# A decoder trunk's attention passes: both groups of scores at the head of a pass, in banks exchanged with the transposes

## The chip, the cores and the metric

One NeuronCore of a Trainium2 chip runs the whole kernel in one launch. Its engines are called here as in the profile: PE (TensorE; its weight loads are PEld), DVE (VectorE), ACT (ScalarE), POOL (GpSimd) and SP (SyncE, which issues loads). The metric is the device time of one execution in microseconds (us), as the median of several. Each engine works through its own queue in order, and an instruction waits at the head of its queue until its semaphores have come.

## What is computed

Two decoder layers on 512 tokens of width 1024 in float32. The first has a gated short convolution, the second sliding-window attention with sinks; each is followed by a SwiGLU block. The change concerns the attention alone: 16 heads of 64, four key heads, and each block of 128 queries sees its own block of keys and the one before.

```python
q = (rmsnorm(h, b_pre_norm[j]) @ b_w_q[j]).reshape(bsz, s, N_HEADS, HEAD_DIM)
q = partial_rotary(q, cos, sin)
attn = sliding_window_sink_attention(q, k_sh, v_sh, b_sinks[j]) @ b_w_o[j]
...
scores = jnp.einsum('bnqhgd,bnkhd->bnhgqk', qb, kk).astype(jnp.float32) * scale
scores = jnp.where(valid[None, :, None, None], scores, NEG)
probs = jax.nn.softmax(jnp.concatenate([scores, sink], axis=-1), axis=-1)[..., :-1]
out = jnp.einsum('bnhgqk,bnkhd->bnqhgd', probs.astype(v.dtype), vv)
```

## The kernel before

Every float32 product is made of three matmuls: each operand is split into a high part (ACT copies it to a shorter float) and a low part (DVE subtracts the high part from the original), and high by low, high by high and low by high are summed in PSUM.

Attention runs over eight head pairs, software-pipelined. The loop at line 1447 makes passes i = 0 to 9, and in each it walks through one string, `ORDER` (line 47). Within the loop the order on PE, DVE, ACT and POOL is the order of the program; a step issues instructions on several engines, and each lands at the end of that engine's queue. A letter is a step, the digit behind it a part of it, and "-" means that it belongs to the pass before. The steps, with pair t = i unless said otherwise:

- R- and H- (pair i + 1): rotate the queries. R: DVE shuffles (`sh`) and multiplies (`ra`), POOL multiplies and adds (lines 1211 to 1215). H: ACT makes the high part `rhi`, POOL the low part `rlo` (lines 1220, 1221). Behind both, POOL issues DMAs that add weight blocks in memory for the next layer (line 535).
- Q0 to Q3 (pair i + 2): project the queries, 6 matmuls of 512 columns each, into one PSUM bank `pq`.
- S0, S1: the scores of two groups of two query blocks each, 12 matmuls with 64-row operands, into two banks `psc` per group (line 1273).
- M0, M1: DVE adds the mask and takes the row maxima, four operations a group (line 1285). The banks of the group are free when these have read them.
- E00, E01, E10, E11: ACT's exponents with row sums (line 1301), and the sink's (line 1308).
- N0, N1: DVE adds sums and sink, takes the reciprocal and scales four pieces (lines 1313 to 1318). The first two pieces of group 0 are 128 wide, the others 256.
- T0 to T3 (pair i - 1): PE transposes the scaled rows into a bank `pt` (line 1330). T0 reads group 0, T1 both groups, T2 and T3 group 1.
- P and L (pair i - 1): ACT's high part `phi` and DVE's low part `plo` of a `pt` bank (lines 1343, 1347).
- W0 to W3 (pair i - 1): weigh the values, 6 matmuls each, into one bank `po`. W of j needs P and L of j.
- O- (pair i - 2): ACT and DVE split the weighed values (`ohi`, `olo`).
- G (pair i + 3): load and split the query weights of a later pair, or, from pass 5 on, of the output projection: ACT makes `whi`, DVE `wlo`, in one step (lines 173 to 188). g0 and g1 do the same for more weights of the output projection, in passes 4 and 6.
- Z and z: from pass 5 on, PE makes two units of the output projection per pass from pairs that are done, and ACT takes their banks.
- K: in pass 2 only, the rotation of the second half of the keys (DVE, POOL, ACT, POOL as for the queries).
- A: in pass 8 only, weights of the next block.

So pass 0 has no T, P, L, W; passes 1 to 5 project queries; passes 6 and 7 don't, but have Z; pass 8 has no scores.

PSUM has eight banks in three pools: four for products (`ps_mm`, with `pq`, `po` and Z), two for the scores (`ps_sc`) and two for the transposes (`ps_pt`). Before the change S0 and S1 both take the two banks of `ps_sc`, so that S1 waits until M0 has read them, and the four transposes take the two banks of `ps_pt` by turns.

Of the kernel before, what the change touches and what calls it, by code (L numbers as in the profile page):

```python
# [10 lines left out]
F32 = mybir.dt.float32  # L11
F32R = mybir.dt.float32r
AF = mybir.ActivationFunctionType
ALU = mybir.AluOpType
PSUM = bass.MemoryType.PSUM

P = 128
D = 1024
S = 512
KT = D // P  # L20
F = 2816
# [23 lines left out]

EARLY_IN, REST_IN = 2, 0
ORDER = (
    "R- T0 g0 S0 O- T1 Q0 M0 Q1 Z0 P0 P1 S1 T2 L0 Q2 L1 G M1 E00 E01 T3 H- Q3 P2 P3 E10 E11 Z1 z0 K W0 L2 L3 A A A N0 W1 W2 N1 W3 g1 z1"
)
STEP = {  # L50
    "S": "scores", "M": "maxima", "E": "exponents", "N": "normalise", "T": "turn", "P": "high",
    "L": "low", "W": "weigh", "O": "out", "Q": "project", "R": "rotate", "H": "split",
    "G": "weights", "Z": "project", "z": "out",
}
N_SLOT, N_WIDE, N_RAW, N_W = 43, 14, 7, 4
EARLY = 4
# [16 lines left out]
def yoco_kernel(  # L73
# [22 lines left out]
    nc = tc.nc  # L96
# [6 lines left out]
    wsp = ctx.enter_context(tc.tile_pool(name="wsp", bufs=N_W))  # L103
# [3 lines left out]
    ps_sc = ctx.enter_context(tc.tile_pool(name="ps_sc", bufs=2, space=PSUM))  # L107
    ps_pt = ctx.enter_context(tc.tile_pool(name="ps_pt", bufs=2, space=PSUM))
# [3 lines left out]
    def name(s):  # L112
        uid[0] += 1
        return f"{s}_{uid[0]}"
# [13 lines left out]
    def bank(s, pool=None):  # L128

        if pool is None:  # L130
            pool = (ps_mm, ps_sc, ps_mm, ps_pt)[turn[0] % 4]
            turn[0] += 1
        return pool.tile([P, S], F32, tag="bank", name=name(s))
# [21 lines left out]
    def fetch(src, n=D):  # L155
        raw = wraw.tile([P, D], F32, tag="raw", name=name("raw"))
        dst = raw[:, :n]
        if len(src.shape) == 3:
            src, dst = src.rearrange("k p c -> p k c"), dst.rearrange("p (k c) -> p k c", c=S)
        nc.sync.dma_start(dst, src)  # L160
        return raw

    class Two:
# [5 lines left out]
        def __getitem__(self, at):  # L169
            h = at[1].start // S  # L170
            return self.of[h][:, at[1].start - h * S : at[1].stop - h * S]

    def split_weights(src, raw=None, slots=False):
        if raw is None:
            raw = fetch(src)
        if slots:
            hi, lo = Two("whi", F32R), Two("wlo", F32R)
            for h in range(2):
                c = slice(h * S, (h + 1) * S)
                nc.scalar.activation(hi[:, c], raw[:, c], AF.Copy)  # L180
                nc.vector.tensor_tensor(out=lo[:, c], in0=raw[:, c], in1=hi[:, c].bitcast(F32),
                                        op=ALU.subtract)
            return hi, lo
        hi = wsp.tile([P, D], F32R, tag="whi", name=name("whi"))
        lo = wsp.tile([P, D], F32R, tag="wlo", name=name("wlo"))
        nc.scalar.activation(hi, raw, AF.Copy)
        nc.vector.tensor_tensor(out=lo, in0=raw, in1=hi.bitcast(F32), op=ALU.subtract)
        return hi, lo
# [468 lines left out]
    with tc.manual_schedule(engines=ALL):  # L657
# [25 lines left out]
        for k in range(KT):  # L683
            pieces = FIRST.get(k, [])
# [6 lines left out]
            for i in range(3):  # L691
                for t in range(3):
                    n = 3 * k + t
                    whi, wlo = (w[:, n % KT * P : (n % KT + 1) * P] for w in ws[n // KT])
# [21 lines left out]
        for b in range(NB):  # L716
            nc.vector.tensor_scalar(out=dg[:, b * P : (b + 1) * P], in0=ident,
                                    scalar1=cols[:, b : b + 1], scalar2=None, op0=ALU.mult)
# [506 lines left out]
    class Queries:  # L1225
# [2 lines left out]
            self.ps = None  # L1228

        def weights(self):  # L1230
            self.w = split_weights(w_q[self.t])

        def project(self, part):
            if part == 0:
# [12 lines left out]
    class Heads:  # L1247
# [11 lines left out]
        def scores(self, half):  # L1259
            khi, klo = ks[self.t // 4]  # L1260
            qhi, qlo = qs[self.t].hi, qs[self.t].lo
            self.pss[half] = pss = [bank("psc", ps_sc) for _ in range(2)]
            for i, cc in self.spans(half):
                n = 2 * half + i
                q = slice(n * P, (n + 1) * P)

                kk = slice(max(n - 1, 0) * P, max(n + 1, 2) * P)
                cc = slice(i * 256, (i + 1) * 256)
                rows = [slice(e * HD, (e + 1) * HD) for e in range(2)]

                for i, (x, y) in enumerate(((qhi, klo), (qhi, khi), (qlo, khi))):
                    for e, r in enumerate(rows):
                        nc.tensor.matmul(pss[e][:, cc], x[r, q], y[r, kk], start=i == 0,
                                         stop=i == 2)
# [35 lines left out]
        def normalise(self, half):  # L1310
            se, rs = self.sums[half]
            pe = self.pe[half]
            nc.vector.tensor_tensor(out=se, in0=se, in1=rs, op=ALU.add)
            rd = small.tile([P, 2, 2], F32, tag="rd", name=name("rd"))
            nc.vector.reciprocal(out=rd, in_=se)
            for i, cc in self.spans(half):
                for e in range(2):
                    nc.vector.tensor_scalar(
                        out=pe[e][:, cc], in0=pe[e][:, cc], scalar1=rd[:, e, i : i + 1],
                        scalar2=None, op0=ALU.mult,  # L1320
                    )

        def turn(self, j):
            pt = bank("pt", ps_pt)
            nq = 2 if j < NB - 1 else 1
            for e in range(2):
                for typ in range(nq):
                    n = j + typ
                    c = (n % 2) * 256 + (P if typ == 0 and n > 0 else 0)
                    nc.tensor.transpose(  # L1330
                        pt[:, (e * nq + typ) * P : (e * nq + typ + 1) * P],
                        self.pe[n // 2][e][:, c : c + P], ident,
                    )
            if nq == 2:
                phi, plo = slot("phi", F32R), slot("plo", F32R)
                self.turned[j] = phi, plo, pt, phi, plo
            else:
                view = [p.rearrange("p (e c) -> p e c", e=2)[:, :, P:] for p in last_p]
                self.turned[j] = *last_p, pt[:, :256].rearrange("p (e c) -> p e c", e=2), *view
# [46 lines left out]
    early_w, rest_w = [], []  # L1386
# [5 lines left out]
    with tc.manual_schedule(engines=ALL):  # L1392
        last_tile(res, [[(0, 4)], [(0, 5)], [], [(0, 6), (0, 7), (1, 0), (1, 1)],
                        [(1, f) for f in (4, 5, 2, 3, 6, 7)]])
        for hf in range(2):
            c = slice(hf * 256, (hf + 1) * 256)
# [41 lines left out]
        src = [p.rearrange("p (h d) -> p h d", d=HD) for p in pv]  # L1438
        for j in range(NB):
            nc.scalar.activation(dst[j][0], src[j], AF.Copy)  # L1440
        for j in range(NB):
            nc.vector.tensor_tensor(out=dst[j][1], in0=src[j], in1=dst[j][0].bitcast(F32),
                                    op=ALU.subtract)

    with tc.manual_schedule(engines=ALL):
        sum_on("a0")
        for i in range(KT + 2):
            if i == KT:
                res = Update(mix_o, B_ATT, [G_FPRE[1]])
                res.leaves = True  # L1450
                ahead = Ahead(first_weights(1))
            if i == KT + 1:
                res.load()
            for c in ORDER.split():
                if c == "A":
                    if i == KT:
                        ahead.one()
                    continue
                if c == "K":
                    if i == 2:  # L1460
                        ks.append(rope_split(rope(pk[1], nc.gpsimd), nc.gpsimd))
                    continue
                late = c.endswith("-")
                op, n = c[0], [int(d) for d in c[1:].rstrip("-")]
                t = i - late
                if op == "g":

                    u = 2 * (t - EARLY - 1) + n[0]
                    if u in (-2, -1, 2, 3):
                        j = u + 2 if u < 0 else u  # L1470
                        early_w.append(split_weights(w_o[j // 2, j % 2], slots=j >= EARLY_IN))
                    continue
                if op in "SMENTPLWO":
                    t -= op in "TPLWO"
                    of = hp
                elif op in "QRH":
                    t += LEAD
                    of = qs
                elif op == "G":
                    t += LEAD + 1  # L1480
                    of = qs
                    if KT <= t < KT + 4:
                        j = t - KT
                        rest_w.append(split_weights(w_o[j // 2, 2 + j % 2], slots=j >= REST_IN))
                else:
                    t = 2 * (t - EARLY - 1) + n.pop(0)
                    of = early
                if 0 <= t < len(of) and not (op in "RH" and t < LEAD - 1):
                    getattr(of[t], STEP[op])(*n)
                if op in "RH" and i <= KT:  # L1490
                    issue(len(issues) // 2 if op == "R" else len(issues))
            if i <= KT:
                sum_on(f"a{i + 1}")
        close(rest_w, at, EARLY, res, ahead, lambda: sum_on(f"a{KT + 2}"), 1)
# [96 lines left out]
```

## Time and profile before

| | us |
|---|---|
| median of 3 runs | 1027.31 (1027.06 to 1027.46) |
| the profiled execution | 1027.09 |
| its span in the trace | 1025.3 |
| PE busy / DVE / ACT / POOL | 1016.4 / 823.7 / 577.4 / 195.8 |
| attention passes 0 to 8 in the span | about 550 to 660 |

The span is what the trace covers, from the first instruction to the last; the profiled execution's own time is 1.8 us more. In rows of the trace in order of time, the columns are start (us from the span's start), duration, engine, line, operation, output and inputs by the program's names, their shapes, a count of merged instructions, and in brackets the idle time of the engine before, with what ended it. Neighbouring instructions of an engine overlap, since they are pipelined: the time that one takes of its engine is read from start to start. PE's ends are modelled, so on PE only starts are used. In rows of stretches the columns are the stretch, its length, busy time and count of PE, PEld, DVE, ACT and POOL, the granted clock, the DMA share and GB/s. In rows of waits they are who waited, for what, the total in us, the times and the longest.

### The profile page before, as it was taken

Reading aid. Unit: us, or ns where it says so; the run is one execution under the profiler, and the core shown is the slowest. Engines: PE = TensorE matmul, PEld = TensorE weight load, DVE = VectorE, ACT = ScalarE, POOL = GpSimd, SP = SyncE. Lnnn points to the kernel's source line nnn. Section 1 sums busy time; section 2 is a strip of 40 time slices with the busy share of each in tenths; the row PEclk is TensorE's granted clock in tenths of the full one; section 3 lists DMA queues with packets and bytes.
Section 4 is the critical chain, followed back from the end, with each engine's and each line's share of the span. In section 5 each row is a group of like instructions: output and inputs, shape, how many; then the busy total and the mean of one; then the engine's idle time right before and its main releaser. Section 6 shows DMA issues by size and latency. Waiting matters only on the chain.

```text
span 1025.3 us, 17466 instructions
## 1 busy us (share of the span) xinstructions
PE 1016.4 (99%) x6648; PEld 925.8 (90%) x6648; DVE 823.7 (80%) x1400; ACT 577.4 (56%) x1035; POOL 195.8 (19%) x259
## 2 busy tenths in 40 slices
PE   9999999999999999999999999999999999999997
PEld 8888888999899898998897888889998999989986
DVE  5766767888688879878869998778886788887786
ACT  7323445865655454566476776677665554645642
POOL 0433033111111111000123653231111010110001
PEclk9999999999999999999999999999999999999999
DMA  9897699459978699779404789976889576988732
GB/s 353 293 268 224 181 255 350 135 169 291 338 246 291 200 313 319 254 220 307 164 9 156 186 246 268 233 280 153 275 282 326 167 263 208 311 286 259 243 135 83
DMA packets 66580, 244.59 MB, mean 239 GB/s; under 512 B 7872, under 2 KB 8384, under 8 KB 54720
## 3 DMA queue, kind: packets, MB, share of 16 engines
q1 hardware_dynamic: 51328, 145.98, 39.0%
q0 software_dynamic: 14592, 96.48, 36.7%
q8 instruction: 52, 0.85, 0.3%
q10 hardware_dynamic: 576, 1.02, 0.3%
q14 instruction: 32, 0.26, 0.1%
HBM read 237.15 MB, written 102.76 MB: 332 GB/s over the span
## 4 chain that ended last, share of the span: by engine, by line
PE 94%; DVE 4%; ACT 1%; DMA 1%; issue 0%; DVEq 0%; SPq 0%
PE gx L193 7%; PE gx L192 7%; PE gx L191 7%; PE gz L192 4%; PE gz L193 4%; PE gz L191 4%; PE pcub L191 4%; PE pcub L193 4%; PE pcub L192 4%; PE px L191 4%; PE px L192 4%; PE px L193 4%; PE pmix L193 3%; PE pmix L191 3%; PE pmix L192 3%; PE gy L191 2%
## 5 line engine op out<-in xcount | busy, mean ns | idle before, releaser
L467 DVE TENSOR_TENSOR wlo<-raw,whi 128x1024 fp32r<-128x1024 f32 x225 | 275.3, 1227 | 93.3 <-ACT whi L466 93.1
L466 ACT ACTIVATE whi<-raw 128x1024 fp32r<-128x1024 f32 x225 | 234.2, 1049 | 118.2 <-DVE raw L454 20.4
L192 PE MATMUL gx<-xt,whi 128*128 128x256 f32 x480 | 135.9, 283 | 0.0
L193 PE MATMUL gx<-xt,wlo 128*128 128x256 f32 x480 | 135.9, 283 | 0.0
L191 PE MATMUL gx<-xt,whi 128*128 128x256 f32 x480 | 135.9, 283 | 0.0
L192 PEld LDWEIGHTS gx<-xt,whi 128*128 128x128 f32 x480 | 92.2, 192 | 0.0
L193 PEld LDWEIGHTS gx<-xt,wlo 128*128 128x128 f32 x480 | 92.2, 192 | 0.0
L191 PEld LDWEIGHTS gx<-xt,whi 128*128 128x128 f32 x480 | 92.2, 192 | 0.0
L535 POOL DMA_DIRECT2D hsum<-in_w_gb_dram x96 | 63.5, 741 | 142.0 <-ACT whi L466 82.3
L1001 ACT ACTIVATE st<-gx 128x256 f32<-128x256 f32 x80 | 30.3, 383 | 82.6 <-PE gx L193 82.6
L535 POOL DMA_DIRECT2D hsum<-hsum x32 | 25.2, 789 | 264.3 <-ACT whi L466 209.1
L192 PE MATMUL pcub<-xhi,whi 128*128 128x512 f32 x168 | 65.4, 389 | 0.0
L191 PE MATMUL pcub<-xlo,whi 128*128 128x512 f32 x168 | 65.4, 389 | 0.0
L193 PE MATMUL pcub<-xhi,wlo 128*128 128x512 f32 x168 | 65.4, 389 | 0.0
L191 PE MATMUL px<-wlo,ahi 128*128 128x512 f32 x120 | 46.7, 390 | 0.0
L192 PE MATMUL px<-whi,ahi 128*128 128x512 f32 x120 | 46.7, 389 | 0.0
L193 PE MATMUL px<-whi,alo 128*128 128x512 f32 x120 | 46.7, 389 | 0.0
L192 PE MATMUL gz<-xt,whi 128*128 128x256 f32 x160 | 45.3, 283 | 0.0
L192 PE MATMUL gx<-xhi,whi 128*128 128x256 f32 x160 | 45.3, 283 | 0.0
L191 PE MATMUL gy<-xlo,whi 128*128 128x256 f32 x160 | 45.3, 283 | 0.0
L192 PE MATMUL gy<-xhi,whi 128*128 128x256 f32 x160 | 45.3, 283 | 0.0
L193 PE MATMUL gz<-xt,wlo 128*128 128x256 f32 x160 | 45.3, 283 | 0.0
(268 smaller groups left out, 3119.7 us busy)
## 6 DMA issues: line engine op xcount, KB each, us to landing
hsum<-in_w_gb_dram POOLq DMA_DIRECT2D x96, 512.0 KB, 8.0
raw<-hsum SPq DMA_DIRECT2D x88, 512.0 KB, 7.9
raw<-in_w_gb_dram SPq DMA_DIRECT2D x60, 512.0 KB, 7.5
hsum<-in_w_dn_dram POOLq DMA_DIRECT2D x36, 512.0 KB, 8.7
raw<-in_w_dn_dram SPq DMA_DIRECT2D x32, 512.0 KB, 6.7
hsum<-hsum POOLq DMA_DIRECT2D x28, 512.0 KB, 5.4
raw<-in_w_in_dram SPq DMA_DIRECT2D x21, 512.0 KB, 8.1
hsum<-in_w_dn_dram POOLq DMA_DIRECT2D x12, 768.0 KB, 12.7
```

The source lines that it names most:

```text
L191: nc.tensor.matmul(out, whi, xlo, start=start, stop=False, **kw)
L192: nc.tensor.matmul(out, whi, xhi, start=False, stop=False, **kw)
L193: nc.tensor.matmul(out, wlo, xhi, start=False, stop=stop, **kw)
L466: self.begun = nc.scalar.activation(hi[:, :n], raw, AF.Copy)
L467: nc.vector.tensor_tensor(out=lo[:, :n], in0=raw, in1=hi[:, :n].bitcast(F32), op=ALU.subtract)
L535: nc.gpsimd.dma_start(dst, src, max_dma_last_dim=4 * 4 * S, **kw))
L1001: nc.scalar.activation(s, x, AF.Copy)
```

## The change

In short:

- S0 and S1 stand together at the head of a pass (in pass 0, S1 stays behind Q0 and Q1). S0 takes the banks of `ps_sc` and S1 those of `ps_pt`; T0 and T1 take `ps_sc`, T2 and T3 `ps_pt`.
- Transposes stand in pairs: T0 T1 behind Q0 and Q1, T2 T3 behind Q2.
- G is cut in two: G loads and makes the high part (ACT), now ahead of the exponents; F makes the low part (DVE), now behind L1. M1 stands right behind E01, ahead of g0 and of all L.
- H- moves ahead of the late exponents; L2 and L3 move ahead of K; W1 moves up to W0.
- Of N0, the two 128-wide scalings run on ACT instead of DVE.

No arithmetic is added or left out. The whole diff:

```diff
--- before.py
+++ after.py
@@ -45,12 +45,12 @@
 
 EARLY_IN, REST_IN = 2, 0
 ORDER = (
-    "R- T0 g0 S0 O- T1 Q0 M0 Q1 Z0 P0 P1 S1 T2 L0 Q2 L1 G M1 E00 E01 T3 H- Q3 P2 P3 E10 E11 Z1 z0 K W0 L2 L3 A A A N0 W1 W2 N1 W3 g1 z1"
+    "R- S0 S1 O- G M0 E00 E01 M1 Q0 Q1 g0 T0 T1 P0 P1 L0 L1 F H- Z0 Q2 T2 T3 E10 P2 P3 L2 L3 E11 Q3 Z1 z0 K W0 W1 A A A N0 W2 N1 W3 g1 z1"
 )
 STEP = {
     "S": "scores", "M": "maxima", "E": "exponents", "N": "normalise", "T": "turn", "P": "high",
     "L": "low", "W": "weigh", "O": "out", "Q": "project", "R": "rotate", "H": "split",
-    "G": "weights", "Z": "project", "z": "out",
+    "G": "high_weights", "F": "low_weights", "Z": "project", "z": "out",
 }
 N_SLOT, N_WIDE, N_RAW, N_W = 43, 14, 7, 4
 EARLY = 4
@@ -169,6 +169,23 @@
         def __getitem__(self, at):
             h = at[1].start // S
             return self.of[h][:, at[1].start - h * S : at[1].stop - h * S]
+
+    def split_begun(src, slots):
+        raw = fetch(src)
+        if slots:
+            w = Two("whi", F32R), Two("wlo", F32R)
+            pieces = [slice(h * S, (h + 1) * S) for h in range(2)]
+        else:
+            w = [wsp.tile([P, D], F32R, tag=tag, name=name(tag)) for tag in ("whi", "wlo")]
+            pieces = [slice(0, D)]
+        for c in pieces:
+            nc.scalar.activation(w[0][:, c], raw[:, c], AF.Copy)
+
+        def rest():
+            for c in pieces:
+                nc.vector.tensor_tensor(out=w[1][:, c], in0=raw[:, c],
+                                        in1=w[0][:, c].bitcast(F32), op=ALU.subtract)
+        return w, rest
 
     def split_weights(src, raw=None, slots=False):
         if raw is None:
@@ -1228,7 +1245,14 @@
             self.ps = None
 
         def weights(self):
-            self.w = split_weights(w_q[self.t])
+            self.high_weights()
+            self.low_weights()
+
+        def high_weights(self):
+            self.w, self.rest = split_begun(w_q[self.t], False)
+
+        def low_weights(self):
+            self.rest()
 
         def project(self, part):
             if part == 0:
@@ -1259,7 +1283,7 @@
         def scores(self, half):
             khi, klo = ks[self.t // 4]
             qhi, qlo = qs[self.t].hi, qs[self.t].lo
-            self.pss[half] = pss = [bank("psc", ps_sc) for _ in range(2)]
+            self.pss[half] = pss = [bank("psc", (ps_sc, ps_pt)[half]) for _ in range(2)]
             for i, cc in self.spans(half):
                 n = 2 * half + i
                 q = slice(n * P, (n + 1) * P)
@@ -1315,13 +1339,15 @@
             nc.vector.reciprocal(out=rd, in_=se)
             for i, cc in self.spans(half):
                 for e in range(2):
-                    nc.vector.tensor_scalar(
-                        out=pe[e][:, cc], in0=pe[e][:, cc], scalar1=rd[:, e, i : i + 1],
-                        scalar2=None, op0=ALU.mult,
-                    )
+                    r = rd[:, e, i : i + 1]
+                    if half == i == 0:
+                        nc.scalar.activation(pe[e][:, cc], pe[e][:, cc], AF.Copy, scale=r)
+                    else:
+                        nc.vector.tensor_scalar(out=pe[e][:, cc], in0=pe[e][:, cc], scalar1=r,
+                                                scalar2=None, op0=ALU.mult)
 
         def turn(self, j):
-            pt = bank("pt", ps_pt)
+            pt = bank("pt", (ps_sc, ps_pt)[j // 2])
             nq = 2 if j < NB - 1 else 1
             for e in range(2):
                 for typ in range(nq):
@@ -1451,7 +1477,10 @@
                 ahead = Ahead(first_weights(1))
             if i == KT + 1:
                 res.load()
-            for c in ORDER.split():
+            order = ORDER
+            if i == 0:
+                order = order.replace("S0 S1", "S0").replace("M1 Q0 Q1", "Q0 Q1 S1 M1")
+            for c in order.split():
                 if c == "A":
                     if i == KT:
                         ahead.one()
@@ -1476,12 +1505,16 @@
                 elif op in "QRH":
                     t += LEAD
                     of = qs
-                elif op == "G":
+                elif op in "GF":
                     t += LEAD + 1
                     of = qs
                     if KT <= t < KT + 4:
                         j = t - KT
-                        rest_w.append(split_weights(w_o[j // 2, 2 + j % 2], slots=j >= REST_IN))
+                        if op == "G":
+                            w, rest = split_begun(w_o[j // 2, 2 + j % 2], j >= REST_IN)
+                            rest_w.append(w)
+                        else:
+                            rest()
                 else:
                     t = 2 * (t - EARLY - 1) + n.pop(0)
                     of = early
```

## The prediction

> **What bounds the kernel now.** I read the page first (busy time by engine, the chain that ended last), then the busy time by stretch inside the attention passes, then the waits, then three engines' rows in order of time.
>
> ```profile
> PE 1016.4 (99%) x6648; PEld 925.8 (90%) x6648; DVE 823.7 (80%) x1400; ACT 577.4 (56%) x1035; POOL 195.8 (19%) x259
> PE 94%; DVE 4%; ACT 1%; DMA 1%; issue 0%; DVEq 0%; SPq 0%
> 570.70:582.90 12.20, 12.20 (x89) 10.28 (x87) 12.12 (x35) 8.81 (x28) 8.77 (x8) 1.00 0.90 247
> 570.90:585.55 14.65, 14.58 (x107) 11.98 (x106) 14.50 (x41) 10.34 (x31) 10.06 (x9) 1.00 0.92 241
> 585.55:596.40 10.85, 10.47 (x69) 8.84 (x68) 10.71 (x38) 8.54 (x26) 5.98 (x6) 1.00 0.61 154
> PEld pt L1330 <- DVE s L1318: 1.3, 4, 0.4
> ```
>
> The stretches give length, then busy time of PE, PEld, DVE, ACT, POOL, then the clock. The first is pass 2 as PE lives it (from its first transposes to the next pass's): 12.2 us without a wait at full clock. The next two are passes 2 and 3 as DVE lives them, from one `sh` of the queries to the next: DVE is busy 14.50 of 14.65 us and 10.71 of 10.85. So PE sets the end of the kernel (94% of the chain), but in passes 2 to 4 DVE has nothing to spare. Time that PE saves here reaches the end only if DVE can follow.
>
> PE's time in a pass holds change-overs between the scores (64-row operands), the transposes and the projections. Pass 4, first as it begins, then where a projection meets the scores in pass 0, then two waits:
>
> ```profile
> 596.18 0.60 PE L1330 MATMUL pt<-ident,s 128*128 128x128 f32 x4
> 596.71 0.38 PE L1273 MATMUL psc<-rlo,rhi 64*128 64x256 f32 x2
> 596.93 0.28 PE L1273 MATMUL psc<-rhi,rhi 64*128 64x256 f32 x2
> 597.05 0.28 PE L1273 MATMUL psc<-rhi,rlo 64*128 64x256 f32 x2
> 597.40 0.28 PE L1273 MATMUL psc<-rhi,rlo 64*128 64x256 f32 x2
> 597.61 0.66 PE L1330 MATMUL pt<-ident,s 128*128 128x128 f32 x4
> 598.03 0.48 PE L191 MATMUL pq<-xlo,whi 128*128 128x512 f32 x1
> 598.34 0.40 PE L192 MATMUL pq<-xhi,whi 128*128 128x512 f32 x1
> 598.58 0.40 PE L193 MATMUL pq<-xhi,wlo 128*128 128x512 f32 x1
> ...
> 555.04 0.28 PE L1273 MATMUL psc<-rhi,rlo 64*128 64x256 f32 x2
> 555.24 0.50 PE L191 MATMUL pq<-xlo,whi 128*128 128x512 f32 x1
> 555.58 0.40 PE L192 MATMUL pq<-xhi,whi 128*128 128x512 f32 x1
> ...
> 588.54 0.76 PE L1273 MATMUL psc<-rlo,rhi 64*128 64x256 f32 x2 [0.33 <-DVE nm L1285]
> 601.27 0.76 PE L1273 MATMUL psc<-rlo,rhi 64*128 64x256 f32 x2 [0.22 <-DVE nm L1285]
> ```
>
> From start to start: four transposes take 0.42 us (597.61 to 598.03), but 0.53 ahead of scores (596.18 to 596.71): 0.11. A pair of score matmuls takes 0.12, the first 0.22: 0.10. So scores cost 0.21 going in. Going out, the last pair takes 0.21 ahead of a transpose (0.09), and ahead of a projection 0.20 with the projection's first matmul at 0.34 for 0.24 (0.18 together). The first projection matmul behind transposes takes 0.31 for 0.24 (0.08 with rounding).
>
> [...]
>
> **The change, part by part.** *Change-overs.* Before, a pass of 1 to 5 goes into scores twice and out to transposes twice, and three times from transposes to a projection: 2 x 0.30 + 3 x 0.08 = 0.84. After: in once, out to a projection once, two transposes-to-projection: 0.21 + 0.18 + 0.16 = 0.55. That saves 0.29 in each of five passes. Passes 6 and 7 have no queries to project: 0.76 becomes 0.46, saving 0.30 each. Together 2.0 us. The way from weighing to scores isn't in the trace; between 0 and 0.2 in, I take the same 0.21, as from transposes.
>
> *Waits of PE that go.* Transposes wait for the normalised rows four times, 1.3 us; scores wait for DVE's maxima 0.33 and 0.22, with some 0.3 more each, since their first matmuls run stretched (0.76). About 0.4 in pass 1, 1.0 in pass 3, 0.5 in pass 4, and 0.4 in pass 8, which stays, because pass 8 has no scores or projections to put ahead of T0.
>
> *What is waited for instead.* T0 and T1 now take the banks of S0, free when M0 has read them, 4.55 us after the pass's head (0.21 + 1.40 for 24 score matmuls + 0.18 + 12 x 0.23 for Q0 and Q1); in passes 6 and 7, without Q0 and Q1, 1.7 us after it. T2 and T3 take the banks of S1, freed by M1 well before them. So DVE's place decides. Its pass 3, with ACT's rows that go with it:
>
> ```profile
> 585.55 0.74 DVE L1211 STREAM_SHUFFLE sh<-pq 128x512 f32<-128x512 f32 x1
> 586.18 0.67 DVE L1213 TENSOR_TENSOR ra<-pq,ctab 128x512 f32<-128x512 f32 x1
> 586.78 0.68 DVE L1365 TENSOR_TENSOR olo<-po,ohi 128x512 fp32r<-128x512 f32 x1
> 587.37 0.34 DVE L1285 CUSTOM_DVE_ANT_0 s<-psc,mask,nsnk 128x128 f32<-128x128 f32 x1
> 588.72 1.28 DVE L1347 TENSOR_TENSOR plo<-pt,phi 128x512 fp32r<-128x512 f32 x2
> 589.92 1.22 DVE L187 TENSOR_TENSOR wlo<-raw,whi 128x1024 fp32r<-128x1024 f32 x1
> 591.05 0.48 DVE L1285 CUSTOM_DVE_ANT_0 s<-psc,mask,nsnk 128x256 f32<-128x256 f32 x1
> 592.67 0.68 DVE L1347 TENSOR_TENSOR plo<-pt,phi 128x512 fp32r<-128x512 f32 x1
> 593.61 0.15 DVE L1313 TENSOR_TENSOR se<-se,rs 128x4 f32<-128x4 f32 x1
> 595.34 1.14 DVE L1318 TENSOR_SCALAR s<-s,rd 128x256 f32<-128x256 f32 x4
> ...
> 585.52 0.60 ACT L1343 ACTIVATE phi<-pt 128x512 fp32r<-128x512 f32 x1 [0.98 <-PE pt L1330]
> 586.01 1.05 ACT L186 ACTIVATE whi<-raw 128x1024 fp32r<-128x1024 f32 x1
> 587.76 0.40 ACT L1301 ACTIVATE s<-s,nm 128x128 f32<-128x128 f32 x1 [0.69 <-DVE nm L1285]
> 589.90 0.62 ACT L1220 ACTIVATE rhi<-ra 128x512 fp32r<-128x512 f32 x1
> ```
>
> Start to start: `sh` 0.63, `ra` 0.60, `olo` 0.59, M0 1.35, L 0.60, weights' low part 1.13, M1 1.62, L2 with L3 0.94, N0 with N1 2.79 (to 596.40). The change takes the two 128-wide scalings of N0 off DVE, 0.45, onto ACT, which has room (8.54 busy of 10.85).
>
> *The low part of the weights meets GpSimd.* DVE's operations on two SBUF operands, and its scalings, don't run beside a GpSimd tensor operation:
>
> ```profile
> 597.22 1.27 POOL L1214 TENSOR_TENSOR sh<-sh,stab 128x512 f32<-128x512 f32 x1 [3.93 <-DVE sh L1211]
> 597.62 1.95 DVE L187 TENSOR_TENSOR wlo<-raw,whi 128x1024 fp32r<-128x1024 f32 x1
> 590.60 1.69 POOL L1221 TENSOR_TENSOR rlo<-ra,rhi 128x512 fp32r<-128x512 f32 x1 [0.86 <-ACT rhi L1220]
> 578.12 0.73 DVE L1211 STREAM_SHUFFLE sh<-pk 128x512 f32<-128x512 f32 x1
> 580.26 1.04 DVE L1313 TENSOR_TENSOR se<-se,rs 128x4 f32<-128x4 f32 x1
> 581.56 1.90 DVE L1318 TENSOR_SCALAR s<-s,rd 128x128 f32<-128x128 f32 x4
> ```
>
> `wlo` at 597.62 took 1.95 for 1.22: it began behind `sh` and ran when that had ended. At 590.60 it is the other way round, `rlo` took 1.69 instead of 1.3 behind a `wlo` begun at 589.92. Now count from M0's start: the exponents begin at 0.39 and fill ACT for 2.14 (587.76 to 589.90); P0 ends at 3.13, P1 begins at 3.02 (0.49 apart, 585.52 to 586.01), `rhi` runs from 3.51 to 4.13, `rlo` from 4.20 to 5.50. DVE: M0 and M1 to 2.97, L0 behind P0 from 3.17, L1 from 3.77, the low part F at 4.37, that is 0.17 behind `rlo`. So F is held to 5.50. Bounds: 0 (F first) and 1.3; I take 1.13 in passes 1 to 4. A DVE pass is then 10.85 - 0.45 + 1.13 + 0.2 = 11.7, PE's 11.9.
>
> *K in pass 2.* The keys' rotation (1.22 on DVE, three GpSimd operations of 1.3 with a 0.62 `rhi`) moves behind L2 and L3. Before, it held N0 and N1 up by 0.9 three times (1.04 for 0.15; 1.90 for 1.0; similarly N1), with L2 and L3 as cover. After, DVE comes to pass 2 at 571.8 (570.90 and pass 1's held F, less N0's share); M0 573.6, L1 done 578.0, F 580.2, L3 581.2, K 582.4; GpSimd's three end at 583.3, 584.7 and 586.7, the scalings of N1 at 587.8. Before: 585.55.
>
> *Passes one by one.* Pass 1: -0.3 - 0.4, and W2, which needs L2 behind F, waits 0.6: -0.1. Pass 2: -0.3. Pass 3: T0 is due at 582.4 + 4.55 = 587.0, its bank is free at 587.8 + 1.82 + 1.02 = 590.6: a wait of 3.6, and W2 waits 0.5 for L2; -0.3 - 1.0 + 4.1 = +2.8. Pass 4 (two more weights on DVE): W2 waits 0.8: -0.3 - 0.5 + 0.8 = 0. Pass 5: DVE comes 2.4 behind PE's head, T0 waits 0.6: +0.3. Passes 6 and 7: from the last weighing to the free bank lie `ohi` 0.67, `olo` 0.64 and three reductions 1.02, 2.35 in all; T0 is due at 1.7: +0.65 - 0.3 each, +0.8 with 0.1 for DVE's lag in 7. Pass 8: 0. Sum: -0.1 - 0.3 + 2.8 + 0 + 0.3 + 0.8 = **+3.5 us**. The profiled execution took 1027.09, 0.2 under the median shown, so 1030.6 and for the median **1030.8**. Bounds of pass 3's wait: 0 if DVE arrives as early as PE, 4.5 if POOL's DMA issues (0.5 to 0.8 each) delay K's operations.
>
> **Rivals.** *F wins its race* (0.17 us decides). Then W2's waits go (0.6 + 0.5 + 0.8 = 1.9), DVE leaves pass 2 some 1.9 earlier (0.9 from pass 1, 1.0 from its own F), and pass 5's wait goes (0.6): 4.4 less, 1026.4. For it: the margin is smaller than one reduction. Against: all its terms are steady rows, and the order is the same in each pass. [...]
>
> *DVE follows and the kernel is faster.* M0 and M1 stand ahead of the weights' low part, the transposes' waits are covered and ACT takes 0.45. If T0 never waits, the change-overs (2.0) and the waits (1.9) are gained: 1023.4. It decides where M0's first bank is free within 4.55 us of PE's head in pass 3, and 1.7 in 6 and 7; rows speak against both.
>
> *GpSimd's queue makes the queries late.* `rlo` stands behind DMA issues that wait for sums; S0 now stands at the very head. If one `rlo` comes 2 us late, 1033. Against: `rlo` ends some 4 us before the next head.
>
> **Chances.** Forecast 0.60, F's race 0.24, faster 0.12, GpSimd 0.04. A measurement of this kernel tells about 0.2%, 2.05 us, from no change. Faster 0.12 (the second rival), same 0.24 (the first), slower 0.64. The range runs from 1025.8, which takes in the first rival, to 1032.8; the second and half of the third are left out. The forecast's own range is 1029.0 to 1032.8.
>
> **What would show it.** Change-overs: score groups of 24 without a gap, one 0.34 projection behind them. F: `wlo` of 1.9 to 2.4 us in passes 1 to 4 with `rlo` just ahead. Pass 3: transposes wait over 2 us for maxima. Passes 6 and 7: T0 waits 0.6 or more. Wrong, if `wlo` takes 1.2 and `rlo` waits instead, or if PE goes through pass 3 without a wait over 1 us.

## The result, and the profile after

The changed kernel takes 1031.47 us (median of 5, 1030.9 to 1033.24), the kernel before on the same chip 1027.19 (5 runs, 1027.06 to 1027.46): a ratio of 1.0043, 95% interval 1.0031 to 1.0054. It is 4.3 us slower. The profiled execution took 1030.9, with a span of 1029.1.

The page after: busy time by engine, and the chain that ended last.

```profile
PE 1015.6 (99%) x6648; PEld 928.0 (90%) x6648; DVE 822.4 (80%) x1384; ACT 581.1 (56%) x1051; POOL 193.9 (19%) x259
PE 92%; DVE 6%; ACT 1%; issue 1%; DVEq 0%; ACTq 0%
```

PE is busy for 0.8 us less and still sets the end, but DVE's share of the chain rose from 4% to 6%: PE now waits for DVE somewhere. To find it, cut both executions at the heads of the passes, the first matmul behind the last weighing (T0 before, S0 after). The stretches of passes 2, 3, 4 and 6, before:

```profile
570.72:582.88 12.16, 12.16 (x88) 10.24 (x87) 12.08 (x34) 8.79 (x28) 8.77 (x8) 1.00 0.89 245
582.88:596.18 13.30, 12.85 (x88) 10.55 (x88) 13.09 (x46) 10.09 (x29) 7.27 (x7) 1.00 0.68 159
596.18:608.90 12.72, 12.45 (x88) 10.45 (x87) 12.58 (x40) 9.66 (x28) 8.74 (x9) 1.00 0.75 182
...
626.36:638.34 11.98, 11.98 (x89) 10.30 (x88) 11.84 (x38) 10.51 (x32) 4.44 (x5) 1.00 0.98 232
```

and after:

```profile
571.45:583.20 11.75, 11.75 (x87) 10.37 (x86) 11.67 (x33) 8.36 (x27) 6.81 (x7) 1.00 0.80 216
583.20:599.88 16.68, 13.46 (x89) 11.64 (x88) 16.26 (x47) 10.36 (x32) 8.74 (x9) 0.90 0.66 169
599.88:611.63 11.75, 11.75 (x87) 10.37 (x86) 11.06 (x33) 10.45 (x31) 7.50 (x9) 1.00 0.70 173
...
629.33:641.88 12.55, 11.72 (x87) 10.36 (x87) 11.56 (x36) 12.16 (x36) 4.22 (x6) 1.00 0.87 229
```

Passes 2 and 4 run without a wait, 11.75 us each. Pass 3 takes 3.4 us more than before, and its mean clock is 0.90. All passes, in us, beside the forecast (pass 8 to the next layer's first matmul):

| pass | before | after | difference | forecast |
|---|---|---|---|---|
| 0 and 1 | 20.26 | 20.27 | 0.0 | -0.1 |
| 2 | 12.16 | 11.75 | -0.4 | -0.3 |
| 3 | 13.30 | 16.68 | +3.4 | +2.8 |
| 4 | 12.72 | 11.75 | -1.0 | 0 |
| 5 | 17.46 | 17.70 | +0.2 | +0.3 |
| 6 and 7 | 24.09 | 25.30 | +1.2 | +0.8 |
| 8 | 10.29 | 9.89 | -0.4 | 0 |
| sum | | | +3.1 | +3.5 |

The other 0.7 us of the profiled difference lies ahead of the attention: the first scores of pass 0 start at 550.46 before and at 551.18 after. The last section gives the reason for putting this down to the execution and not to the change.

The 0.0 of passes 0 and 1 hides terms that cancel. In pass 1 the changed kernel's W2 waits 0.28, and T0 waits 0.37 (0.60 from the last projection matmul, which needs 0.23), for which the prediction had no term.

PE in pass 3 after, in order of time, and the clock in three stretches of 4 us:

```profile
587.45 0.39 PE L210 MATMUL pq<-xhi,wlo 128*128 128x512 f32 x1
591.07 1.94 PE L1356 MATMUL pt<-ident,s 128*128 128x128 f32 x8 [3.23 <-DVE nm L1309]
592.66 0.78 PE L208 MATMUL pq<-xlo,whi 128*128 128x512 f32 x1
593.23 0.63 PE L209 MATMUL pq<-xhi,whi 128*128 128x512 f32 x1
593.66 0.63 PE L210 MATMUL pq<-xhi,wlo 128*128 128x512 f32 x1
594.09 0.47 PE L208 MATMUL pq<-xlo,whi 128*128 128x512 f32 x1
```

```profile
587.00:591.00 4.00, 0.84 (x4) 0.38 (x2) 4.00 (x15) 1.53 (x4) 2.26 (x3) 0.98 0.28 78
591.00:595.00 4.00, 3.94 (x16) 3.50 (x17) 3.86 (x13) 4.00 (x15) 1.98 (x3) 0.60 0.60 98
595.00:599.00 4.00, 4.00 (x31) 3.74 (x30) 3.86 (x10) 3.06 (x12) 1.52 (x3) 1.00 0.69 201
```

The transposes T0 and T1 start 3.62 us behind the last projection matmul, which needs 0.23: a wait of 3.39 for the maxima that free the bank. Then the matmuls run at half pace: 1.59 for the eight transposes that take some 0.8 elsewhere, 0.43 for a projection matmul of 0.23. The granted clock, 0.98 ahead, is 0.60 for these 4 us. Pass 3's own sum is 16.68 - 11.75 - 3.39 = 1.54 us for the slow clock.

What DVE did meanwhile, from the weights' low part of pass 2 to pass 3's maxima, and GpSimd beside it:

```profile
578.59 2.21 DVE L186 TENSOR_TENSOR wlo<-raw,whi 128x1024 fp32r<-128x1024 f32 x1
...
581.66 0.73 DVE L1228 STREAM_SHUFFLE sh<-pk 128x512 f32<-128x512 f32 x1
...
582.88 0.96 DVE L1337 TENSOR_TENSOR se<-se,rs 128x4 f32<-128x4 f32 x1
...
584.09 1.51 DVE L1346 TENSOR_SCALAR s<-s,rd 128x256 f32<-128x256 f32 x2
...
585.92 2.25 DVE L1346 TENSOR_SCALAR s<-s,rd 128x256 f32<-128x256 f32 x4
588.09 0.01 DVE L1228 LOAD_MASK_SELECT sh<-pq  x1
...
590.43 0.48 DVE L1309 CUSTOM_DVE_ANT_0 s<-psc,mask,nsnk 128x256 f32<-128x256 f32 x1
```

```profile
578.43 1.28 POOL L1238 TENSOR_TENSOR rlo<-ra,rhi 128x512 fp32r<-128x512 f32 x1 [1.79 <-ACT rhi L1237]
...
582.54 1.29 POOL L1231 TENSOR_TENSOR sh<-sh,stab 128x512 f32<-128x512 f32 x1 [1.27 <-DVE sh L1228]
583.90 1.28 POOL L1232 TENSOR_TENSOR ra<-ra,sh 128x512 f32<-128x512 f32 x1
585.93 1.29 POOL L1238 TENSOR_TENSOR rlo<-ra,rhi 128x512 fp32r<-128x512 f32 x1 [0.74 <-ACT rhi L1237]
```

Read the two side by side. F begins at 578.59, 0.16 behind `rlo`, and takes 2.21 instead of 1.22: it lost its race. K's three GpSimd operations each hold a VectorE operation: `se` takes 0.96 for 0.15, the scalings of N0 1.51 for 0.62, those of N1 2.25 for 1.14. DVE leaves pass 2 at 588.09, and the third reduction of pass 3, which frees T0's bank, starts at 590.43, takes 0.48 and is over 0.16 ahead of T0's start.

### The profile page after: what moved, and what is told of

Read it like the earlier page. It is cut to its first block, busy times and chain, and to the rows that moved or that the text cites. A ratio compares the mean times of both kernels' runs of the same rounds, so it can differ in the third digit from the quotient of the medians.

```text
span 1029.1 us, 17456 instructions
## 1 busy us (share of the span) xinstructions
PE 1015.6 (99%) x6648; PEld 928.0 (90%) x6648; DVE 822.4 (80%) x1384; ACT 581.1 (56%) x1051; POOL 193.9 (19%) x259
## 3 DMA queue, kind: packets, MB, share of 16 engines
q10 hardware_dynamic: 576, 1.02, 0.3%
## 4 chain that ended last, share of the span: by engine, by line
PE 92%; DVE 6%; ACT 1%; issue 1%; DVEq 0%; ACTq 0%
PE gx L210 7%; PE gx L209 7%; PE gx L208 7%; PE gz L210 4%; PE gz L209 4%; PE gz L208 4%; PE pcub L208 4%; PE pcub L209 4%; PE pcub L210 4%; PE px L208 4%; PE px L209 4%; PE px L210 4%; PE pmix L210 3%; PE pmix L208 3%; PE pmix L209 3%; PE gy L209 2%
## 5 line engine op out<-in xcount | busy, mean ns | idle before, releaser
L210 PE MATMUL gx<-xhi,wlo 128*128 128x256 f32 x160 | 45.3, 283 | 0.0
L210 PE MATMUL gy<-xhi,wlo 128*128 128x256 f32 x160 | 45.3, 283 | 0.0
```

The lines of the kernel that those rows point to most:

```text
L210: nc.tensor.matmul(out, wlo, xhi, start=False, stop=stop, **kw)
```

## The experiments

All are compared with the changed kernel's 1031.47. The edits of the order are shown as the part of the string that differs. The kernel before took 1027.5 to 1027.6 on the chips of these runs, and 1027.19 where the changed kernel was measured, so that a difference from 1031.47 is uncertain by some 0.4 us. The changed kernel's five runs also spread over 2.3 us, and its trace is of the shortest. Where a difference is about 1 us, the length of passes 0 to 8 in the traces stands beside it, from the first scores to the next layer's first matmul: 113.34 us in the changed kernel, 110.28 in the one before.

**The low part of the weights first.** F moves from behind L1 to directly behind M1, ahead of `rlo`.

```diff
-M1 Q0 Q1 g0 T0 T1 P0 P1 L0 L1 F H-
+M1 F Q0 Q1 g0 T0 T1 P0 P1 L0 L1 H-
```

> The changed kernel, with F (DVE's low part of the weights) directly behind M1 instead of behind L1. F is then due 2.97 us after M0's start, ahead of the GpSimd low part of the queries (4.20), which waits for F instead. Theory, F is held by GpSimd and DVE's lost microseconds pile up to pass 3: wlo takes 1.2 us instead of 2.2 to 2.3 in passes 1 to 3, the transposes' wait of 3.4 us in pass 3 falls to 1.2 to 2.5 us, PE's clock stays at 1.0 there (the changed kernel shows 0.60 in 591 to 595), and the median falls by 2.5 to 5 us, to 1026.5 to 1029. Rival, DVE has simply too much ahead of M0 in a pass and F's place is no matter: L0 and L1 come later by what F gains, within 0.5 us of 1031.5.

Measured: 1028.56 (10 runs, 1027.09 to 1029.22), ratio to before 1.0008 (0.9998 to 1.0017). DVE, then GpSimd, in pass 2 of this kernel:

```profile
575.69 1.22 DVE L186 TENSOR_TENSOR wlo<-raw,whi 128x1024 fp32r<-128x1024 f32 x1
```

```profile
577.22 1.30 POOL L1238 TENSOR_TENSOR rlo<-ra,rhi 128x512 fp32r<-128x512 f32 x1 [2.09 <-ACT rhi L1237]
```

F takes 1.22, and `rlo` behind it isn't disturbed. T0's wait in pass 3 falls to 2.45, the waits of W2 are gone, pass 5's falls from 0.45 to 0.22. Losing the race costs the change 2.9 us: without it the kernel is level with the one before. The traces' passes agree (110.21, 3.1 less), but 1.54 of these 3.1 is the slow clock, which doesn't come in this trace. It is of one of three runs at 1027.1 to 1027.2; the other seven took 1028.4 to 1029.2.

**Z0 as cover.** The output projection's unit, which only passes 5 to 8 have, moves ahead of T0.

```diff
-g0 T0 T1 P0 P1 L0 L1 F H- Z0 Q2
+g0 Z0 T0 T1 P0 P1 L0 L1 F H- Q2
```

> The changed kernel, with Z0 (2.74 us of PE work from pass 5 on) ahead of T0 instead of behind T1. Theory, in passes 5 to 7 T0 waits for M0 to free the banks of S0 because nothing stands between scores and transposes: the waits of 0.4, 1.0 and 1.2 us go, and the time falls by 2.0 to 2.7 us, to about 1029. Rival, the wait only moves: without Z0 behind the transposes, W or the next pass waits for P and L instead, and the time stays within 0.5 us.

Measured: 1028.66 (10 runs, 1027.49 to 1029.46), 1.0009 (0.9999 to 1.0018). In pass 6 the scores go straight over into the projection and from there into the transposes:

```profile
629.53 0.28 PE L1297 MATMUL psc<-rhi,rlo 64*128 64x256 f32 x2
629.74 0.50 PE L208 MATMUL pe<-wlo,ohi 128*128 128x512 f32 x1
...
632.37 0.39 PE L210 MATMUL pe<-whi,olo 128*128 128x512 f32 x1
632.60 0.60 PE L1356 MATMUL pt<-ident,s 128*128 128x128 f32 x4
```

The waits of passes 5 to 7 (0.45 + 0.98 + 1.14 = 2.6 in the changed kernel) are gone, and 2.8 us with them (2.15 by the traces' passes, 111.19). Pass 3 stays as it was: a wait of 3.38, then a clock of 0.57 in 591 to 595.

**K earlier, and a projection ahead of T0.** In the first kernel K stands ahead of L2 and L3, in the second Q2 stands ahead of T0, in pass 3 only.

```diff
-P2 P3 L2 L3 E11 Q3 Z1 z0 K W0
+P2 P3 K L2 L3 E11 Q3 Z1 z0 W0
```

> The changed kernel, with K (rotation of the second half of the keys, pass 2) ahead of L2 and L3 on DVE again. Theory, K's three GpSimd operations hold up N0 and N1 longer in the changed kernel because L2 and L3 no longer cover them: DVE leaves pass 2 about 0.9 us earlier, T0's wait in pass 3 falls from 3.4 to about 2.5 us, the clock falls less or not, and the time by 0.9 to 2.5 us, to 1029 to 1030.6. Rival, W2 of pass 2 then waits some 1.2 us for L2 and pass 3 begins that much later: no gain, within 0.5 us.

```diff
+            if i == 3:
+                order = order.replace("Q2 T2", "T2").replace("g0 T0", "Q2 g0 T0")
```

> The changed kernel, with Q2 (1.4 us of PE work) ahead of T0 in pass 3 alone; nothing else moves. Theory, the long wait also costs clock: after 3.4 us of idleness PE ran at 0.60 for 4 us, some 1.5 us lost. With 2.0 us of idleness the clock stays at 1.0 in pass 3; DVE's chain to L2 then ends the pass, so of the 2.9 us that PE could save (1.4 moved into the wait, 1.5 of clock) about 1 to 1.5 us remain: 1030 to 1030.5. Rival, the clock doesn't hang on the wait: 0.6 again in that stretch, and a gain under 0.5 us.

Measured: 1030.03 (10 runs; 1.0024, 1.0015 to 1.0034) and 1030.41 (8 runs; 1.0024, 1.0013 to 1.0035). PE with K early:

```profile
582.55 0.39 PE L208 MATMUL po<-plo,vt 128*128 128x256 f32 x1 [0.86 <-DVE plo L1373]
...
590.64 1.06 PE L1356 MATMUL pt<-ident,s 128*128 128x128 f32 x8 [1.83 <-DVE nm L1309]
```

K early takes 1.40 off T0's wait (1.99 from start to start, for 3.39), but W2 of pass 2 now waits 1.02 for L2, which stands behind K. Theory and rival are both in the trace, so that K's move itself nets 0.4. The medians show a gain of 1.4, the passes of the traces (113.07) one of 0.3: the slow clock, 1.54, doesn't come, but W2 waits 0.33 and 0.77 in passes 3 and 4 in its stead. With Q2 ahead of T0, the wait falls to 2.04, but T2 then waits 0.63, and the clock falls to 0.59 all the same, so that the part of the expectation on the clock was wrong. The median of 1030.41 lies in the expected range, but not for its reason, and the passes (113.32) show no gain at all.

**Both moves that worked.** F behind M1 and Z0 ahead of T0.

> The changed kernel with both moves: F directly behind M1 and Z0 ahead of T0. Alone, the first took 2.9 us off the changed kernel and the second 2.8. Theory, they act at different places (passes 1 to 4, passes 5 to 7) and add: 5 to 5.7 us off 1031.5, 1025.8 to 1026.5, the first version that is faster than before; left is a wait of about 2.4 us in pass 3. Rival, both only absorb one and the same lag of DVE: the sum gives 3 to 4 us, 1027.5 to 1028.5.

Measured: 1027.18 (10 runs, 1025.18 to 1027.66), 0.9992 (0.9982 to 1.0001). They add to 4.3 us, less than the 5.7 of their sum; the time lies between the two expectations. Three runs lie at 1025.2 to 1025.6, seven at 1026.7 to 1027.7; the profiled one, 1027.56, has a wait of 2.45 in pass 3 and then 0.61 of the clock, where the kernel with F alone kept 1.00 behind the same wait.

**K out of pass 2 as well.** To the last kernel's moves this adds K in pass 3, whose keys are needed later: behind E01, ahead of M1.

```diff
-G M0 E00 E01 M1 Q0 Q1 g0 T0 T1 P0 P1 L0 L1 F H- Z0 Q2
+G M0 E00 E01 K M1 F Q0 Q1 g0 Z0 T0 T1 P0 P1 L0 L1 H- Q2
...
-                    if i == 2:
+                    if i == 3:
```

> As the kernel with both moves, and K (keys' rotation, due only in pass 4) in pass 3 between E01 and M1, where DVE works on PSUM (M1, L0, L1) while GpSimd rotates, instead of pass 2 ahead of N0. Theory, what is left of pass 3's wait is K holding up N0 and N1 in pass 2: T0's wait of 2.4 us in pass 3 falls under 0.5, W2 of pass 3 waits up to 1 us for L2, and 1.2 to 2.4 us are gained on the kernel with both moves: 1023.5 to 1025. Rival, the lock moves with K: F in pass 3 waits for it and pass 3 or 4 loses the same 2 us, within 0.5 us of the kernel with both moves.

Measured: 1023.96 (5 runs, 1023.79 to 1024.54), 0.9966 (0.9953 to 0.9979). It beats both kernels, the one before by 3.6 us. Its stretches of passes 2 to 4 and 6, and PE in pass 3:

```profile
571.13:582.88 11.75, 11.75 (x87) 10.37 (x87) 10.99 (x40) 9.06 (x29) 6.16 (x6) 1.00 0.92 249
582.88:595.67 12.79, 12.01 (x87) 10.32 (x86) 11.37 (x34) 9.57 (x30) 9.70 (x9) 1.00 0.82 180
595.67:607.52 11.85, 11.85 (x87) 10.29 (x86) 11.68 (x37) 10.21 (x31) 7.57 (x9) 1.00 0.66 161
...
624.73:636.47 11.74, 11.74 (x89) 10.40 (x88) 10.61 (x36) 11.49 (x35) 4.57 (x6) 1.00 1.00 247
```

```profile
587.13 0.39 PE L210 MATMUL pq<-xhi,wlo 128*128 128x512 f32 x1
587.36 1.03 PE L1356 MATMUL pt<-ident,s 128*128 128x128 f32 x8
...
594.05 0.38 PE L208 MATMUL po<-plo,vt 128*128 128x256 f32 x1 [0.78 <-DVE plo L1373]
```

T0 follows the projection at once, and the clock stays at 1.00. What is left of waits in pass 3 is W2's, 0.94. Each of these passes is shorter than before, by 0.24 (pass 6) to 0.87 (pass 4).

**All of N0 on DVE.** The changed kernel without ACT's two scalings.

```diff
-                    if half == i == 0:
+                    if False:
```

> The changed kernel with all of N0's scalings on DVE as before the change. Theory, DVE sets the end in passes 1 to 4, so the 0.45 us a pass that ACT had taken over come back and pile up to pass 3: its wait grows from 3.4 to about 4.3 us, passes 4 to 7 wait a little longer, and the time grows by 1 to 2.5 us, to 1032.5 to 1034. Rival, the scalings hide behind the waits of PE: within 0.5 us of 1031.5.

Measured: 1033.02 (4 runs, 1032.69 to 1033.15), 1.0052 (1.0035 to 1.0068). The waits grow: T0 of pass 1 to 0.76, W2 of pass 4 to 1.15, T0 of pass 5 to 1.0, of pass 7 to 1.58. T0 of pass 3 waits 3.51, and yet the stretch behind keeps its clock:

```profile
591.00:595.00 4.00, 3.43 (x23) 3.06 (x24) 3.85 (x17) 4.00 (x16) 2.10 (x3) 1.00 0.47 66
```

So ACT's scalings are worth 1.55 us to the change by the medians, and 2.45 by the passes of the traces (115.79), although the slow clock is missing here.

**PE kept busy through the wait.** Twelve matmuls of 512 columns ahead of T0 in pass 3, into a bank that nobody reads.

```diff
+                if c == "T0" and i == 3:
+                    fill = bank("fill", ps_mm)
+                    for _ in range(12):
+                        nc.tensor.matmul(fill, ones_r, xq[0][0], start=True, stop=True)
```

> The changed kernel with twelve added matmuls of 512 columns ahead of T0 in pass 3, into a bank that is read by nobody (the output is unchanged): some 2.8 us of the 3.4 us in which PE would sit idle. Theory, the clock of 0.60 behind that wait comes from the idleness: with the wait filled the granted clock stays at 1.0 in 591 to 595, the eight transposes take 0.9 us instead of 1.7, and since DVE's L2 then ends the pass about 1 us is gained: 1030.3 to 1030.9. Rival, the clock falls for another reason: 0.6 again, and the time within 0.3 us of 1031.5 or later by a part of the 2.8.

Measured: 1030.82 (5 runs, 1030.19 to 1032.1), 1.0033 (1.002 to 1.0046). T0 starts when it did, PE waits only 0.59, and the clock is 1.00:

```profile
587.63 2.97 PE L1495 MATMUL fill<-xhi,ones_r 128*128 128x512 f32 x12
591.03 1.06 PE L1356 MATMUL pt<-ident,s 128*128 128x128 f32 x8 [0.43 <-DVE nm L1309]
```

Of the 1.54 us that the slow clock stretched PE's work, the medians give 0.65 back, which is within the spread of the runs, and the traces nothing: passes 0 to 8 take 113.31 us, for 113.34. So the time lies in the expected range without the expected gain. The 1.54 turned into waits for DVE: W2 waits 0.33 in pass 3 and 0.75 in pass 4, T0 0.62 in pass 5, where the changed kernel's trace has none, none and 0.45. Nor does this one trace show that the filling kept the clock up: the kernel with N0 on DVE kept it behind an open wait.

**K alone, and K in the kernel of before.** The changed kernel with K in pass 3 and nothing else; and the kernel of before with K there and ACT's two scalings.

```diff
-R- S0 S1 O- G M0 E00 E01 M1 Q0 Q1
+R- S0 S1 O- G M0 E00 E01 K M1 Q0 Q1
```

> The changed kernel with K alone taken out of pass 2 and issued in pass 3, behind the upper scores' transposes and ahead of M1; F and Z0 stay as the change has them. Theory (T0 of pass 3 waits for N0 of pass 2, and N0 and N1 of pass 2 are late chiefly because K's GpSimd operation holds VectorE): T0's wait falls from 3.4 us to under 1.0, the granted clock in 591 to 595 stays at 1.00, and the time falls by 2 to 3.5 us from 1031.5, to 1028 to 1029.5. Rival (the delay moves along with K: VectorE is held in pass 3 instead, and W2 of pass 3 and T0 of pass 4 wait for it): within 0.7 us of 1031.5.

```diff
-L0 Q2 L1 G M1 E00 E01 T3 H- Q3 P2 P3 E10 E11 Z1 z0 K W0
+L0 Q2 L1 G E00 E01 K M1 T3 H- Q3 P2 P3 E10 E11 Z1 z0 W0
```

> The kernel of before with what the best version does for VectorE: K moved from pass 2 to pass 3, between the upper scores' transposes and M1, and N0's two 128-wide scalings on ScalarE. Theory (merging the scores is worth about 2 us of change-overs, and moving K is worth the waits of before in passes 3 and 4, 1.5 us): 1025 to 1026.5, with the best version still 1.5 to 2.5 us ahead. Rival (all of the best version's gain comes from moving K): 1024.0 or less. Second rival (the order of before does not need K moved, its waits come from elsewhere): 1027 to 1028.

Measured: 1029.55 (10 runs, 1029.16 to 1030.35; 1.0020, 1.0010 to 1.0029) and 1029.59 (10 runs, 1029.09 to 1029.99; 1.0021, 1.0012 to 1.0031). The first, in pass 3:

```profile
593.29 0.38 PE L208 MATMUL po<-plo,vt 128*128 128x256 f32 x1 [0.74 <-DVE plo L1373]
...
596.64 0.39 PE L208 MATMUL po<-plo,vt 128*128 128x256 f32 x1 [1.66 <-DVE plo L1373]
```

T0's wait is gone and the clock is 1.00, as the theory has it, but W0 and W2 of the same pass now wait 0.90 and 1.81 for the low parts, W2 also 0.75 in pass 4. The result lies between the two expectations: K's delay moved along by half. The best kernel, which up to pass 4 differs from this one in F's place alone (Z0 acts from pass 5 on), has only W2's 0.94 left there. K's new place pays with F ahead of `rlo`: there the move took 3.2 us off (1027.18 to 1023.96), here 1.9.

In the kernel of before the same place, with the scalings on ACT, costs 2.1 us, which none of the three expectations had. ACT in pass 3, then PE in passes 1 and 3:

```profile
593.43 1.15 ACT L1220 ACTIVATE rhi<-ra 128x512 fp32r<-128x512 f32 x2 [3.52 <-POOL ra L1215]
594.49 0.58 ACT L1345 ACTIVATE phi<-pt 128x512 fp32r<-128x512 f32 x1
```

```profile
559.93 0.73 PE L1332 MATMUL pt<-ident,s 128*128 128x128 f32 x4 [0.90 <-ACT s L1320]
...
595.84 0.38 PE L191 MATMUL po<-plo,vt 128*128 128x256 f32 x1 [1.01 <-DVE plo L1349]
```

K's `rhi` stands at the head of ACT's queue for 3.52 us until GpSimd has rotated the keys; `phi` stands behind it, and the weighing waits for the low part made from it, 1.16 from start to start. The scalings cost too: on ACT they stand behind the late exponents, and T0, which comes first in a pass here, waits for them 1.06 in pass 1 and 0.64 in pass 4. Passes 0 and 1, ahead of K, are 0.65 longer than before. So this run, with two edits at once, doesn't tell how much of the best kernel's gain is change-overs; the lengths of its passes 2 and 6 do.

## Why the prediction came out as it did

**Direction and mechanism were right; several terms were mis-sized and cancel.** PE saves change-overs, transposes now take banks that DVE frees late, and DVE's place in pass 3 decides. By the steps as put:

- *Change-overs, 0.29 a pass.* In undisturbed passes the best kernel saves 0.41 in pass 2 and 0.24 in pass 6. Of the 0.41, 0.15 is no change-over: T0 came late at the end of that stretch before (0.27 behind a weighing matmul that takes 0.12). The size holds.
- *F is held 1.13 in passes 1 to 4.* The changed kernel's F in passes 1, 3 and 4 (pass 2 stands above):

```profile
566.96 2.21 DVE L186 TENSOR_TENSOR wlo<-raw,whi 128x1024 fp32r<-128x1024 f32 x1
594.29 2.31 DVE L186 TENSOR_TENSOR wlo<-raw,whi 128x1024 fp32r<-128x1024 f32 x1
...
607.62 1.55 DVE L186 TENSOR_TENSOR wlo<-raw,whi 128x1024 fp32r<-128x1024 f32 x1
```

  Right in passes 1 to 3; `rlo` had begun at 566.80, 578.43 and 594.24, so the margin forecast as 0.17 us was 0.16, 0.16 and 0.05. In pass 4 `rlo` had begun 0.82 earlier (606.80), and only its remainder was waited for. Moving F ahead gave 2.9 (by the medians) of the 4.4 us that the rival had put on the race: it took 0.94 off T0's wait in pass 3, not 1.9, and of W2's waits there was less to win than the 1.9 put on them.
- *K holds N0 and N1; DVE leaves pass 2 at 587.8; T0 of pass 3 waits 3.6.* Measured 588.09, with a start-up 0.73 later, and 3.39. Moving K ahead of L2 took 1.40 off that wait, moving it to pass 3 all of it.
- *W2 waits 0.6 in pass 1, 0.5 in pass 3, 0.8 in pass 4.* Over-sized: 0.28, 0 and 0 in the changed kernel. In passes 3 and 4 the slow clock stands in their place: it delayed PE by 1.54, so that PE came too late to wait. With the clock at 1.00, the filled kernel shows 0.33 and 0.75. Most of the miss of pass 4 (-1.0) and of pass 3 (+0.6) is this.
- *Passes 6 and 7, 0.65 each.* Under-sized: 0.90 and 1.06. Rows of pass 6, ACT's `ohi`, then PE's last weighing matmul and its transposes:

```profile
629.43 0.60 ACT L1390 ACTIVATE ohi<-po 128x512 fp32r<-128x512 f32 x1 [2.27 <-PE po L210]
```

```profile
629.12 0.28 PE L210 MATMUL po<-lp,vt 128*128 128x256 f32 x1
...
631.84 1.06 PE L1356 MATMUL pt<-ident,s 128*128 128x128 f32 x8 [0.83 <-DVE nm L1309]
```

  The weighing's last matmul takes 0.12 of PE, so that it is over at 629.24. T0 starts 2.60 behind that and not 2.35: `ohi` begins 0.19 later, which the chain of durations had left out. Against the due time as put, 1.7 behind the weighing, the wait is 0.90 (in pass 7, worked out alike, 1.06). The 0.98 and 1.14 given with Z0 count from the end of the last pair of score matmuls by its pace of 0.12, and so hold the change-over out of the scores too.
- *Pass 8, 0.* It got 0.4 shorter: T0's wait there, taken as staying, went.

**The slow clock** was in no step of the prediction. It took the place of the 0.5 + 0.8 us of waits for DVE that were forecast; in the filled kernel waits of that kind (0.33 and 0.75) come in its stead, and passes 0 to 8 take as long (113.31 us for 113.34). Where DVE is the bound, a slower PE cost next to nothing here. That the sum came out so near (+3.1 for +3.5) is luck in part: passes 3, 4, 6 with 7, and 8 missed by +0.6, -1.0, +0.4 and -0.4, which nearly cancel.

Of the rivals, the first is refuted by the rows of F, and so is the second by the wait of 3.39; its price of 1023.4 is nearly what the best kernel reaches (1023.96), where the transposes of pass 3 no longer wait. The third named `rlo` ahead of S0; no scores wait for it in the changed kernel.

## What to carry to other kernels

When an engine that sets the end is freed of waits, list for each bank that changes hands who frees it now, and follow that engine's queue back through the pass before: here the places of one subtraction, one rotation and one projection decided between 4.3 us lost and 3.6 us won. Two operations that held each other up (`wlo` took 2.21 us behind `rlo` and 1.22 ahead of it) shouldn't come up within 0.2 us of one another, where the order of one queue decides about 1 us in each of passes 1 to 3. Work that needs nothing of the pass (a projection of finished pairs) belongs ahead of the wait, where it covers it.

## What the runs showed of the hardware

**The granted clock fell behind a wait of 2.45 us in one execution, and stayed at 1.00 behind one of 3.51 in another.** The wait of T0 in pass 3 and the clock of 591 to 595: 3.39 and 0.60 (the change), 3.38 and 0.57 (Z0 first), 2.45 and 0.61 (both moves); with Q2 first 0.59, behind 2.04 and T2's further 0.63; but 3.51 and 1.00 (N0 on DVE), 2.45 and 1.00 (F first), 1.99 and 1.00 (K early). Length alone doesn't decide. Nor does the pace always fall where the wait ends: with Z0 first and with both moves, T0 and T1 still run at full pace behind it (0.82 us for eight), and the projection matmuls behind them at 0.43 for 0.23. It probably differs between runs of one kernel: of F first, the three runs at 1027.1 to 1027.2 had a mean clock of 0.998, the seven others 0.996 or 0.997, so that the clock probably fell in those; no trace of them shows it. What decides whether the clock falls was not shown.

**The first scores of pass 0 start at 550.4 to 550.5 in four executions and at 550.8 to 551.6 in eight.** Among the early ones are the kernel of before and three of the change's order, among the late ones the change and, at 551.18, the order of before with K moved. Up to there the kernel before and its order with K moved have the same order, and yet differ by 0.7. So up to 1.2 us of a profiled difference here is probably the execution's (no kernel was traced twice), and passes should be compared from a common point of the program.

**`wlo` on DVE and `rlo` on GpSimd held each other up, whichever began first.** In pass 2 of the changed kernel F took 2.21 us behind an `rlo` begun 0.16 earlier. In the kernel before `rlo` took 1.69 behind a `wlo` begun 0.68 earlier. With F first they stood apart (575.69 and 577.22) and took 1.22 and 1.30. Why they did was not shown.
